# Cumulative decays, query latent and modulation blocks issued elsewhere in a two-layer hybrid diffusion backbone

## Chip, cores, metric

One core of a Trainium2 chip runs the whole program in one launch. The metric is the device time of that launch in microseconds (us). It is stated as the median of several runs.

## What is computed

The reference is a backbone of two layers (here called layer 0 and layer 1) over 512 latent tokens and 256 context tokens of width 1024. Cut to what the change touches, one layer is:

```python
mx = (silu(c) @ w_ada + b_ada)            # six modulation vectors: shift, scale, gate, twice
h  = rms_norm(x) * (1 + scale) + shift
p  = h @ w_in                             # columns: query latent, key/value latent, neighbourhood q k v,
                                          # DeltaNet q k v, gate z, two decay and two beta columns per head
mla = softmax_attention(rms_norm(q_latent) @ w_q_up, rms_norm(kv_latent) @ w_kv_up, ...)
na  = neighbourhood_attention(nq, nk, nv, bias)
q, k, v = silu(depthwise_conv(...));  g = -exp(a_log) * softplus(a + dt_bias)
gc  = cumsum(g) in each chunk             # decays exp(gc), exp(gc_last - gc), exp(gc_last)
dn  = gated_delta_rule(l2norm(q), l2norm(k), v, g, beta), both directions
dn  = rms_norm(dn) * silu(z)
x   = x + gate * (concat(mla, na, dn) @ w_out);   then a SwiGLU block with its own modulation
```

The context tokens go through the same weights in layer 0. In layer 1 they only serve as keys and values.

## The kernel before

Every matrix product with a large weight runs on TensorE in three passes of a rounded high part and a low part (`gemm`, L341). A weight tile of 128 output columns is loaded from memory into a buffer `wr`, split on ACT (`wh`, L216) and POOL (`wl`, L217), and multiplied with eight blocks of the normalised input (`hh`, `hl`). Two buffers of each exist. For the 512 latent columns a tile costs 24 matmuls of 512 columns, for the 256 context columns 24 of 256. The results of the input projection lie in three PSUM banks: two for latent accumulators (`x512`) and one for context accumulators (`x256`), so a second context product waits until the first one is read.

The source is written in an order of stages, and the Tile framework's scheduler then fixes the order of the instructions on each engine before the run. It walks a timeline of its own; where several instructions of an engine are ready on it, the one written earlier goes first. On the chip each engine runs its list in that order: an instruction that waits holds everything behind it. `tc.issue_after(x)` adds one constraint: the instructions in its block come behind `x` on the engine of `x`.

The stages of a layer, in the order in which they are written:

- the decay and beta columns (`TILE_AB`, L513), and from them `g`, a chain of some thirty small instructions on DVE and ACT, among them a series in L538 to L540. Its last step is L547.
- the cumulative decays (L553 to L563): five small fp32 products of `g` with constant triangles into one bank `gc`, two instructions each on PE, and five exponentials on ACT that give `egc`, `etail` and `egl`. The first reader is L620 in `gates`; the others are read in the scan.
- four key projections with their convolution (`conv("k", h)`, L484, L591), then the norms of the keys (`norms`, L568), the query and value projections with `gates` between them, the neighbourhood projections, and a triangular inverse in blocks.
- the tail (L977 to L986), an order written by hand in `TAIL` (L46): `z` is one gate tile (`do_z`, L786: projection, tanh on ACT, product on DVE at L791, a transfer of `z` to memory at L794), `k` the key/value latent (`do_kv`), `q` the query latent (`do_ql`, L762: two tiles, squares, their sum `sqs` on DVE at L771, six products with ones into `ms_q`, then the scale of the queries by L778, L780 to L783). The tanh of the last `z` is followed by a load of the activation table that holds ln and exp (`preload`, L182). Behind the tail the pools of the input (`h`), of the convolution buffers (`cvp`, which also holds `sqs`, `sq`, `thz` and `z`) and of the projection banks are closed, and others take their place.
- neighbourhood attention in 12 blocks in layer 0 and 8 in layer 1 (`attention`, L843). Ahead of each block `beside` (L1095) issues some steps of the DeltaNet scan and inverse (`DNS`), and in layer 0 two modulation blocks (`ADA`, L37). Then come the latent attention, the output projection and the SwiGLU block.

A modulation block (`ada_cols`, L220) loads 512 KB of `w_ada` into `wada`, multiplies it with the condition in eight products (`acc_ada`), copies the result to SBUF (`adarow`, L231, one buffer), and turns it into columns with a product per 128 values (`tr_ada`), to which DVE adds the bias (L236). In the first part of layer 0 four pairs of such calls stand ahead of the first norm; the 24 blocks beside the attention give the parts 2, 4 and 3, which are read from the output projection on.

POOL and DVE meet behind the tail: POOL prepares the block inverse with four products `Y` of 1024 columns (L941), DVE transposes strips (L925, L935) and does the softmax steps.

## Time and profile before

| | us |
|---|---|
| median of 3 runs | 2143.08 |
| lowest and highest run | 2142.63, 2143.99 |
| the profiled execution's own time | 2144.62 |
| its span, first to last instruction | 2142.5 |
| PE busy in the span | 1997.7 (93%) |
| DVE, ACT, POOL busy | 1178.1, 707.3, 839.9 |

PE is TensorE's matmuls, PEld its weight loads (they overlap PE), DVE is VectorE, ACT ScalarE, POOL GpSimd, SPq the queue of SyncE that issues transfers. A timeline row tells the start of an instruction from the span's start, its length, engine, source line, what it writes and reads, its shape, how many like it are merged, and in brackets how long its engine sat idle before it and which instruction released it. Every matrix product has the line of the helper, L104, so these are told apart by their tiles. The granted clock is the share of TensorE's full speed (1.00 is 2.4 GHz, 0.50 is 1.2 GHz) in a stretch.

### The profile page before, as it was taken

To read this page: it belongs to the slowest core of one execution; us is meant where nothing else is said; L and a number is where in the kernel's file an instruction comes from. 1 tells how busy PE (TensorE), PEld (TensorE's weight loads), DVE (VectorE), ACT (ScalarE), POOL (GpSimd) and SP (SyncE) were. 2 spreads that over 40 slices of the span, in tenths; PEclk is the share of its full clock that TensorE was granted. 3 is DMA by queue.
4 is the path that set the end of the run, shared out by engine and by line. 5 is a ranking of instruction groups with operands and counts; after the bars stand their busy time and mean duration, and the time that the engine had idled before them with its cause. 6 is when DMAs were issued, how large, how long until landed. Compare 5 with 4: busy or idle time off the path is not lost. (4 is left out here: it accounts for less than half of the span.)

```text
span 2142.5 us, 32149 instructions
## 1 busy us (share of the span) xinstructions
PE 1997.7 (93%) x12770; PEld 1692.0 (79%) x12770; DVE 1178.1 (55%) x2045; ACT 707.3 (33%) x1381; POOL 839.9 (39%) x664
## 2 busy tenths in 40 slices
PE   6899898998998999999999988868899889999998
PEld 4788687887787888888888876757787678888887
DVE  4889813667757457246344358893478654212123
ACT  5433223334544221122122344323344543222233
POOL 3467733103332222322222443884302352444444
PEclk9999998999999999999999999989899999999999
DMA  7324242443322334234432331334222232333332
GB/s 277 82 80 136 100 127 95 150 147 125 106 62 79 108 124 168 93 128 135 131 118 81 121 87 59 123 109 119 94 77 77 82 99 69 95 93 94 102 96 91
DMA packets 119278, 232.57 MB, mean 109 GB/s; under 512 B 30484, under 2 KB 55956, under 8 KB 119000
## 3 DMA queue, kind: packets, MB, share of 16 engines
q1 hardware_dynamic: 119128, 230.51, 34.1%
q8 instruction: 101, 1.65, 0.3%
q14 instruction: 49, 0.40, 0.1%
HBM read 199.46 MB, written 31.01 MB: 108 GB/s over the span
## 5 line engine op out<-in xcount | busy, mean ns | idle before, releaser
L217 POOL TENSOR_TENSOR wl<-wr,wh 128x1024 fp32r<-128x1024 f32 (+2 forms) x188 | 439.8, 2340 | 773.7 <-ACT wh L216 750.3
L216 ACT CAST wh<-wr 128x1024 fp32r<-128x1024 f32 (+2 forms) x190 | 193.6, 1019 | 730.1 <-PE acc_gu L104 289.4
L104 PE MATMUL acc_gu<-fh,wh 128*128 128x512 f32 (+1 forms) x1024 | 358.8, 353 | 9.6 <-ACT fh L304 8.7
L104 PE MATMUL acc_gu<-fl,wh 128*128 128x512 f32 (+1 forms) x1024 | 360.5, 353 | 4.1 <-DVE fl L305 4.1
L104 PE MATMUL acc_gu<-fh,wl 128*128 128x512 f32 (+1 forms) x1024 | 359.5, 352 | 0.0
L104 PE MATMUL acc_in<-hh,wh 128*128 128x512 f32 (+1 forms) x640 | 230.9, 365 | 25.3 <-DVE nkl L703 8.6
L104 PE MATMUL acc_in<-hl,wh 128*128 128x512 f32 (+1 forms) x640 | 230.3, 361 | 3.2 <-DVE hl L305 2.0
L104 PE MATMUL acc_in<-hh,wl 128*128 128x512 f32 (+1 forms) x640 | 227.3, 360 | 2.3 <-POOL wl L217 2.1
L104 PEld LDWEIGHTS acc_gu<-fh,wh 128*128 128x128 f32 x1024 | 193.9, 190 | 37.5 <-ACT fh L304 11.0
L1344 DVE TENSOR_TENSOR av<-acc_gu,av 128x768 f32<-128x768 f32 (+1 forms) x44 | 36.3, 825 | 337.0 <-PE acc_gu L104 329.8
L104 PEld LDWEIGHTS acc_gu<-fl,wh 128*128 128x128 f32 x1024 | 194.6, 190 | 30.2 <-DVE fl L305 4.3
L104 PEld LDWEIGHTS acc_gu<-fh,wl 128*128 128x128 f32 x1024 | 194.4, 190 | 26.3
L104 PEld LDWEIGHTS acc_in<-hh,wh 128*128 128x128 f32 x640 | 127.2, 200 | 52.8 <-DVE nkl L703 9.9
L104 PE MATMUL acc_d<-al,wh 128*128 128x512 f32 (+1 forms) x444 | 157.2, 354 | 0.0
L104 PE MATMUL acc_d<-ah,wh 128*128 128x512 f32 (+1 forms) x444 | 157.2, 354 | 0.0
L104 PE MATMUL acc_d<-ah,wl 128*128 128x512 f32 (+1 forms) x444 | 156.1, 354 | 0.0
L254 DVE CUSTOM_DVE_ANT_0 junk<-wada,scb 128x1024 f32<-128x1024 f32 x112 | 144.7, 1292 | 7.2 <-DMA wada<-w_adaT 4.4
L104 PEld LDWEIGHTS acc_in<-hl,wh 128*128 128x128 f32 x640 | 127.8, 200 | 24.8 <-DVE hl L305 4.6
L104 PEld LDWEIGHTS acc_in<-hh,wl 128*128 128x128 f32 x640 | 126.5, 200 | 21.0 <-POOL wl L217 3.6
L1362 DVE SCALAR_TENSOR_TENSOR xT<-acc_d,mod,xT 128x512 f32<-128x512 f32 (+1 forms) x76 | 46.5, 634 | 154.6 <-PE acc_d L104 154.6
L501 DVE SCALAR_TENSOR_TENSOR cy<-xp,cw,cy 128x770 f32<-128x770 f32 (+1 forms) x96 | 117.7, 1226 | 22.0 <-ACT cy L499 20.0
L1348 DVE TENSOR_TENSOR al<-av,ah 128x768 fp32r<-128x768 f32 (+1 forms) x44 | 100.4, 2282 | 35.1 <-ACT ah L1347 35.1
(391 smaller groups left out, 3957.8 us busy)
## 6 DMA issues: line engine op xcount, KB each, us to landing
wr<-w_gu SPq DMA_DIRECT2D x88, 512.0 KB, 3.5
wada<-w_adaT SPq DMA_DIRECT2D x56, 512.0 KB, 3.3
wr<-w_in SPq DMA_DIRECT2D x48, 512.0 KB, 3.7
wr<-w_dn SPq DMA_DIRECT2D x32, 448.0 KB, 3.4
wada<-w_ada SPq DMA_DIRECT2D x24, 512.0 KB, 3.3
wada<-w_ada SPq DMA_DIRECT2D x8, 1024.0 KB, 8.4
wr<-w_dn SPq DMA_DIRECT2D x16, 512.0 KB, 3.5
xT<-xT SPq DMA_DIRECT2D x16, 384.0 KB, 5.7
```

The lines of the kernel that those rows point to most:

```text
L104: nc.tensor.matmul(out, lhsT, rhs, start=start, stop=stop)
L216: S.copy(out=hi[:, sl], in_=raw[:, sl])
L217: eng.tensor_tensor(out=lo[:, sl], in0=raw[:, sl], in1=hi[:, sl].bitcast(F32), op=ALU.subtract)
L254: V.tensor_tensor_reduce(out=junk, in0=w, in1=scb[:, s], scale=1.0, scalar=0.0, op0=ALU.mult, op1=ALU.add, accum_out=mod[l][:, part, j, s: ...
L501: stt(out=y[:, :wid], in0=xp[:, j:j + wid], scalar=w_(j), in1=y[:, :wid], op0=ALU.mult, op1=ALU.add)
L1344: tt(out=av[:, :nT], in0=accs[1][:, :nT], in1=av[:, :nT], op=ALU.mult)
L1348: after.append(tt(out=l_[:, :nT], in0=av[:, :nT], in1=h_[:, :nT].bitcast(F32), op=ALU.subtract))
L1362: stt(out=xT[:, m, st_], in0=acc, scalar=mod[l][:, 5, m, s:s + 1], in1=xT[:, m, st_], op0=ALU.mult, op1=ALU.add)
```

## The change

Three edits.

1. The five products of the cumulative decays and their exponentials are written behind the four key projections, and the products are bound behind the last matmul of those projections (`last["mm"]`). This holds in both layers.
2. In layer 0 the tail is `zkqzzz` instead of `zzzzkq`: one gate tile, the key/value latent, the query latent, three gate tiles.
3. A modulation block beside the attention returns its second half (`turn`: `tr_ada`, the bias, and the scale) instead of running it. It is run after the first half of the next block, and bound behind that block's last matmul; the last one runs after the loop. `adarow` has two buffers. The calls ahead of the first norm run both halves at once, as before.

```diff
--- before.py
+++ after.py
@@ -43,7 +43,7 @@
 PRE0, LATE = True, ()
 ROW = lambda S, V: S.copy
 HLP = ([(k, 1) for k in range(8)], [], [(k, 1) for k in (0, 2, 4, 6, 7)], [])
-TAIL = ["zzzzkq", "kzzqzz"]
+TAIL = ["zkqzzz", "kzzqzz"]
 INV = ((3, 4), (5, 2))
 WV = ((6,), (23,))
 MR = 2
@@ -101,7 +101,7 @@
 
 
 def mm(nc, out, lhsT, rhs, start=True, stop=True):
-    nc.tensor.matmul(out, lhsT, rhs, start=start, stop=stop)
+    return nc.tensor.matmul(out, lhsT, rhs, start=start, stop=stop)
 
 
 def mm3(nc, out, l, r, start=True, stop=True):
@@ -226,19 +226,22 @@
         acc = bank("acc_ada")
         for k in range(KD):
             g = 32 * (k % 4)
-            mm(nc, acc[g:g + 32, 0:nb * P].rearrange("p (j c) -> p j c", j=nb), sc[:, k], w[:, :, k], k < 4, k >= 4)
-        row = sb.tile([P, nb * P], F32, tag="adarow", name="adarow", bufs=1)
+            last["ada"] = mm(nc, acc[g:g + 32, 0:nb * P].rearrange("p (j c) -> p j c", j=nb), sc[:, k], w[:, :, k], k < 4, k >= 4)
+        row = sb.tile([P, nb * P], F32, tag="adarow", name="adarow", bufs=2)
         (V.tensor_copy if slot is wp else ROW(S, V))(out=row, in_=acc[:, 0:nb * P])
-        res = bank("tr_ada")
-        for b in range(nb):
-            mm(nc, res[:, 2 * b:2 * b + 2], row[:, b * P:(b + 1) * P], C("sum4"))
-        js = slice(j0, j0 + nb)
-        tt(out=mod[l][:, part, js], in0=res[:, 0:2 * nb].rearrange("p (j s) -> p j s", s=2), in1=bc(bada[:, l, part, js], 2), op=ALU.add)
-        if part in (1, 4):
-            i = part // 4
-            t1 = sb.tile([P, nb, 2], F32, tag="adat", name="adat", bufs=1)
-            V.tensor_scalar(out=t1, in0=mod[l][:, part, js], scalar1=1.0, scalar2=None, op0=ALU.add)
-            tt(out=gs[l][:, i, js], in0=t1, in1=bc(gm[:, l, i, js], 2), op=ALU.mult)
+
+        def turn():
+            res = bank("tr_ada")
+            for b in range(nb):
+                mm(nc, res[:, 2 * b:2 * b + 2], row[:, b * P:(b + 1) * P], C("sum4"))
+            js = slice(j0, j0 + nb)
+            tt(out=mod[l][:, part, js], in0=res[:, 0:2 * nb].rearrange("p (j s) -> p j s", s=2), in1=bc(bada[:, l, part, js], 2), op=ALU.add)
+            if part in (1, 4):
+                i = part // 4
+                t1 = sb.tile([P, nb, 2], F32, tag="adat", name="adat", bufs=1)
+                V.tensor_scalar(out=t1, in0=mod[l][:, part, js], scalar1=1.0, scalar2=None, op0=ALU.add)
+                tt(out=gs[l][:, i, js], in0=t1, in1=bc(gm[:, l, i, js], 2), op=ALU.mult)
+        return turn
 
     def ada_rows(todo, sb, after):
 
@@ -347,7 +350,7 @@
                 o = acc[:, st.start - c0:st.stop - c0]
                 mm(nc, o, wh[:, w], xh[k][:, st], k == 0, False)
                 mm(nc, o, wh[:, w], xl[k][:, st], False, False)
-                mm(nc, o, wl[:, w], xh[k][:, st], False, k == nk - 1)
+                last["mm"] = mm(nc, o, wl[:, w], xh[k][:, st], False, k == nk - 1)
 
 
     es_x = ExitStack()
@@ -399,7 +402,7 @@
 
     if nx is None:
         nx = e.open_norm(l, A_)
-        pre = lambda k: k % 2 or [e.ada_cols(l, p, k, 2, eb, nx.sb, nx.sb) for p in (1, 0)]
+        pre = lambda k: k % 2 or [e.ada_cols(l, p, k, 2, eb, nx.sb, nx.sb)() for p in (1, 0)]
         pre(0)
         rss = e.rstd_of(xT, eb, nx.sb, both)
         for k in range(KD):
@@ -549,18 +552,6 @@
     S.activation(out=beta, in_=ab[:, :, 8:16], func=AF.Exp, scale=-1.0)
     V.tensor_scalar(out=beta, in0=beta, scalar1=1.0, scalar2=None, op0=ALU.add)
     V.reciprocal(out=beta, in_=beta)
-
-    egc, etail, egl = sc6(), sc6(), sc6()
-    tp = eb("gc")
-    gf = g.rearrange("p c x -> p (c x)")
-    for i, nm in enumerate(("u_f", "u_b", "v_f", "v_b", "ones")):
-        mm(nc, tp[:, 48 * i:48 * i + 48], C(nm), gf)
-    tpv = lambda i: tp[:, 48 * i:48 * i + 48].rearrange("p (c x) -> p c x", x=8)
-    for d in range(2):
-        ds_ = slice(4 * d, 4 * d + 4)
-        S.activation(out=egc[:, :, ds_], in_=tpv(d)[:, :, ds_], func=AF.Exp)
-        S.activation(out=etail[:, :, ds_], in_=tpv(2 + d)[:, :, ds_], func=AF.Exp)
-    S.activation(out=egl, in_=tpv(4), func=AF.Exp)
     V.tensor_scalar(out=sml[:, 12:13], in0=sml2[:, 19:20], scalar1=0.5, scalar2=None, op0=ALU.mult)
 
     t2 = lambda nm: sb.tile([P, 512], F32, tag="t2", name=nm, bufs=5)
@@ -590,6 +581,19 @@
 
     for h in range(4):
         conv("k", h, kT[:, h])
+
+    egc, etail, egl = sc6(), sc6(), sc6()
+    tp = eb("gc")
+    gf = g.rearrange("p c x -> p (c x)")
+    with tc.issue_after(e.last["mm"].ins):
+        for i, nm in enumerate(("u_f", "u_b", "v_f", "v_b", "ones")):
+            mm(nc, tp[:, 48 * i:48 * i + 48], C(nm), gf)
+    tpv = lambda i: tp[:, 48 * i:48 * i + 48].rearrange("p (c x) -> p c x", x=8)
+    for d in range(2):
+        ds_ = slice(4 * d, 4 * d + 4)
+        S.activation(out=egc[:, :, ds_], in_=tpv(d)[:, :, ds_], func=AF.Exp)
+        S.activation(out=etail[:, :, ds_], in_=tpv(2 + d)[:, :, ds_], func=AF.Exp)
+    S.activation(out=egl, in_=tpv(4), func=AF.Exp)
     st4, rk = [sb.tile([P, 6, 4], F32, name=nm) for nm in ("st4", "rk")]
     norms("k", t2, st4, rk, True)
     irk = sc3()
@@ -1092,13 +1096,22 @@
 
     ada_bank = lambda name: (psV if ADA_T == "i" else psD).tile([P, 512], F32, tag=ADA_T, name=name, bufs=1)
 
+    turns = []
+
+    def turn_last():
+        if turns:
+            with tc.issue_after(e.last["ada"].ins):
+                turns.pop()()
+
     def beside(ada, sb):
 
         for _ in range(next(dn_n, 16)):
             next(dn, lambda: 0)()
         for _ in range(next(ada, 0) if l == 0 else 0):
             i = next(ada_n)
-            e.ada_cols(0, (2, 4, 3)[i // KD], i % KD, 1, att_bank if ADA_T == "T" else ada_bank, sb, e.wp)
+            turn = e.ada_cols(0, (2, 4, 3)[i // KD], i % KD, 1, att_bank if ADA_T == "T" else ada_bank, sb, e.wp)
+            turn_last()
+            turns.append(turn)
 
 
 
@@ -1106,6 +1119,7 @@
         beside(ada, sn)
         if next(na, None) is None:
             break
+    turn_last()
     es_w.close()
     es_si.close()
     es_na.close()
```

## Rows read from the trace of the kernel before

**Rows 1.** The page's part 1: busy time, share of the span, instructions.

```profile
PE 1997.7 (93%) x12770; PEld 1692.0 (79%) x12770; DVE 1178.1 (55%) x2045; ACT 707.3 (33%) x1381; POOL 839.9 (39%) x664
```

**Rows 2.** Windows at the end of layer 0's projections: length, busy us of PE, PEld, DVE, ACT, POOL, granted clock, DMA.

```profile
290.00:351.00 61.00, 61.00 (x376) 52.69 (x375) 7.20 (x12) 19.98 (x31) 14.33 (x8) 1.00 0.34 110
351.00:370.00 19.00, 11.19 (x67) 9.97 (x65) 13.17 (x32) 3.79 (x14) 10.65 (x7) 0.69 0.39 130
370.00:382.00 12.00, 12.00 (x76) 9.46 (x77) 4.49 (x16) 3.51 (x11) 0.00 (x0) 0.50 0.18 55
382.00:490.00 108.00, 107.91 (x1372) 90.93 (x1371) 72.26 (x237) 35.79 (x123) 13.21 (x21) 1.00 0.49 163
```

**Rows 3.** Timeline, PE, layer 0's seam: start, length, [idle before <- releaser].

```profile
354.75 2.52 PE L104 MATMUL ms_q<-cst,sqs 128*128 128x2 f32 x12 [3.63 <-DVE sqs L771]
357.81 0.56 PE L104 MATMUL tr_ada<-cst,adarow 128*128 128x2 f32 x2 [0.55 <-DVE adarow L231]
...
359.31 2.08 PE L104 MATMUL yp<-vp,Y 128*128 128x128 f32 x8
...
365.54 0.59 PE L104 MATMUL tr_ada<-cst,adarow 128*128 128x2 f32 x2 [3.62 <-DVE adarow L231]
```

**Rows 4.** Timeline, DVE, the same stretch.

```profile
352.19 2.41 DVE L771 TENSOR_TENSOR sqs<-sqs,sq 128x768 f32<-128x768 f32 x1
357.30 0.16 DVE L778 TENSOR_SCALAR sml<-ms_q 128x6 f32<-128x6 f32 x1 [2.70 <-PE ms_q L104]
...
362.10 2.29 DVE L782 TENSOR_SCALAR sml<-sml 128x6 f32<-128x6 f32 x1
...
365.40 0.68 DVE L1031 TENSOR_TENSOR w<-yp,scal 128x512 f32<-128x512 f32 x1
```

**Rows 5.** Timeline, POOL, the same stretch.

```profile
351.45 2.34 POOL L941 TENSOR_TENSOR Y<-strips,cst 128x1024 f32<-128x1024 f32 x1
357.40 6.96 POOL L941 TENSOR_TENSOR Y<-strips,cst 128x1024 f32<-128x1024 f32 x3 [3.61 <-PE ms_q L104]
```

**Rows 6.** Timeline, PE, layer 1's tail and seam.

```profile
1520.43 0.95 PE L104 MATMUL ms_q<-cst,sqs 128*128 128x2 f32 x8
...
1542.42 1.11 PE L885 MATMUL tp_na<-cst,pr 128*128 128x128 f32 x4 [4.07 <-DVE pr L880]
```

**Rows 7.** Windows, layer 1's seam (columns as in rows 2).

```profile
1529.00:1546.00 17.00, 9.34 (x60) 7.68 (x59) 14.47 (x24) 6.05 (x14) 12.15 (x8) 0.70 0.40 131
```

**Rows 8.** Timeline, ACT, the last gate tile of layer 0.

```profile
324.86 0.38 ACT L790 ACTIVATE thz<-acc_in 128x256 f32<-128x256 f32 x1
325.26 1.28 ACT L182 ACT_TABLE_LOAD   x1
```

**Rows 9.** The tile z of layer 0: its vector step, and its transfer to memory.

```profile
L791 DVE SCALAR_TENSOR_TENSOR z<-thz,acc_in x8: 420/554/691, 297.0 to 325.3; 128x512 f32<-128x512 f32 x4, 128x256 f32<-128x256 f32 x4
...
DMA to landing us min/median/max: 2.8/3.1/3.1
```

**Rows 10.** Timeline, ACT, layer 1's tail: an activation table.

```profile
1522.18 1.28 ACT L781 ACT_TABLE_LOAD   x1
```

**Rows 11.** Timeline, PE, layer 0's key projections.

```profile
79.13 1.31 PE L104 MATMUL gc<-scal,cst 128*128 128x48 f32 x10 [0.98 <-DVE scal L547]
81.73 0.48 PE L104 MATMUL acc_in<-hh,wh 128*128 128x256 f32 x1 [1.29 <-ACT xp L495]
```

**Rows 12.** Windows of layer 0 behind the key projections (columns as in rows 2).

```profile
84.00:136.00 52.00, 51.32 (x277) 40.81 (x277) 38.98 (x52) 24.81 (x39) 16.96 (x24) 0.99 0.18 61
136.00:262.00 126.00, 111.50 (x627) 93.63 (x626) 118.15 (x156) 36.32 (x57) 105.93 (x113) 0.95 0.34 111
```

**Rows 13.** Timeline, PE, layer 1: the cumulative decays.

```profile
1292.69 0.28 PE L104 MATMUL acc_in<-hh,wl 128*128 128x256 f32 x1
1292.81 0.40 PE L104 MATMUL acc_in<-hh,wh 128*128 128x512 f32 x1
...
1308.42 2.37 PE L104 MATMUL gc<-scal,cst 128*128 128x48 f32 x10 [6.68 <-DVE scal L547]
```

## The prediction

> **What bounds the kernel.** I read the page's shares first, then TensorE's waits stage by stage, then the timelines of the other engines in the stretches where it waits, and last the granted clock there. PE is busy 93% of the span [rows 1], so a change of order can win only what PE idles or runs at half clock. Most stages leave nothing: in layer 0's tail PE is busy 61.00 of 61 us at clock 1.00, and in the attention stretch 107.91 of 108 [rows 2]. Between them lies a seam. From 351 to 370 us PE is busy 11.19 of 19 us at a mean clock of 0.69, and from 370 to 382 it has no gap but runs wholly at 0.50 [rows 2]. That makes 7.8 us idle, and 2 x 0.31 x 19 + 12 = 23.8 us at 1.2 GHz. All three edits should be read against this seam and against one stall in layer 1.
>
> In the seam PE waits 3.63 us for `sqs`, runs `ms_q` at half clock in 2.52 us, waits 0.55 and later 3.62 us for `adarow` [rows 3]. Behind `ms_q` hang others too: POOL's last three `Y` wait for it 3.61 us [rows 5], because `sqs` lies in memory that they take over. In layer 1 PE stands 6.68 us before the decays [rows 13].
>
> **The query latent moves ahead of three gate tiles.** The same matmuls run, in another order.
> - The wait for `sqs` (3.63 us) goes: the sum on DVE takes at most 2.41 us [rows 4], and a gate tile's projection stands behind it, a seventh of the tail's 61 us or 8.7 us of PE work [rows 2]. Layer 1 already has gate tiles behind its query latent, and there `ms_q` starts without an idle bracket [rows 6]. Gain 3.6 us. If the scheduler places `ms_q` before that cover, the wait stays.
> - `ms_q` itself runs at full clock: eight took 0.95 us in layer 1 [rows 6], so twelve take 1.4 instead of 2.5. Gain 1.1.
> - Something else is last now. Behind the last gate matmul come tanh of the context part (0.38 us), the table load (1.28) [rows 8] and DVE's product (0.42) [rows 9]; only then are the bank and the buffers free. In the old order all three lay under the latents' projections. The sum is 2.1 us; if the next stage needs only the bank, without the load, it is 0.8; if it needs memory that `z` holds until its transfer lands (3.1 us [rows 9]), it is 0.4 + 0.4 + 3.1 = 3.9, plus the loads of the scan, which SP issues in order behind this transfer. I take 2.1, since the freed resource nearest to the first rows of the seam is the bank and ACT must load the table before its first exp.
> - ln and exp of the two latents now lie between tanh steps. In layer 1, where they do, exp cost another load of 1.28 us [rows 10]. Up to five more loads are 6.4 us of ACT, which is busy only 19.98 of the tail's 61 us [rows 2]: nothing, as long as the casts of the next weights are not the ones delayed; then 1.28 each.
> - The transfers of three gate tiles and the weight loads move with their steps on SP; seven weight tiles are loaded before and after. Nothing.
>
> **The modulation blocks.** 24 blocks issue the same instructions. The first wait (0.55) goes, since the next block's eight products stand before the turn. The second (3.62) is only partly the block's own: the `adarow` copy stood on DVE behind L782, which took 2.29 us, and L1031, which PE's next step needs, ended only at 366.1 [rows 4]. L782 belongs to the query latent and leaves the seam with it. So of 3.62 I count 2.3. Together 2.9 us; bounds 0.5 and 4.2. In the 108 us behind the seam PE has 0.1 us of idle time [rows 2], so the other blocks win nothing there; the second `adarow` is only memory. Each turn takes a bank of the attention's three one block later; I count nothing, and up to 0.1 us for each of 24 if a score tile has to wait for it, 2.4 in all.
>
> **DVE against POOL.** L782 has six columns. The like-shaped L778 took 0.16 us, L782 2.29, inside POOL's three `Y` from 357.40 to 364.36 [rows 4, 5]. In layer 1 a transpose waits 4.07 us for DVE's `pr`, in a seam where POOL is busy 12.15 of 17 us [rows 6, 7]. With `ms_q` gone, the three `Y` no longer wait 3.61 us, and meet the first softmax steps. I add 1.5 us, between 0 and the 4.07 of layer 1, nearer the low end because the steps they meet are few.
>
> [...]
>
> **The clock.** The 12.00 us of work behind the seam at 0.50 would take about 6 at full clock. In layer 1's seam 2 x 0.30 x 17 = 10.2 us are at half clock [rows 7], against 23.8 here. With less idle time I expect about half of that difference, 6.8 us less at 1.2 GHz, worth some 3.0 us. Bounds 0 and 6.
>
> **The decays.** In layer 0 `gc` stands in a hole that stays: PE waits 0.98 us, runs 1.31, and waits 1.29 for ACT's `xp`, which does not depend on it [rows 11]. Moved behind the projections, the 1.31 us lands in a stretch where PE is busy 51.32 of 52 us [rows 12]. Behind that, DVE is the fuller engine (118.15 of 126 us, PE 111.50), so part is taken up. I add 0.7; bounds 0 and 1.3. The exponentials are first read in `gates`, which comes behind the projections in either order. In layer 1 the last context matmul of the key projections is issued at 1292.69, and other projections follow it before `gc` [rows 13]. So `gc` is already behind them there; the new bound is met by the old order, `g` comes no earlier, and I count 0 of the 6.68.
>
> **Sum**: -3.6 - 1.1 + 2.1 - 2.9 + 1.5 - 3.0 + 0.7 = -6.3 us. Against the profiled execution's 2144.62 that is 2138.3; the median stands 1.54 lower, so 2143.08 - 6.3 = 2136.8, said as **2137.0**. 0.2%, about what a measurement can tell from no change, is 4.3 us: faster means below 2138.8, slower above 2147.4.
>
> **Rivals.**
> 1. *Layer 1's stall goes too.* If writing `gc` later makes the scheduler put more query projections before it, the 6.68 us is covered, and `gc` runs in 1.31 instead of 2.37 us [rows 11, 13]: 7.7 more, 2129. For it: work is there, since projections resume right after. Against: nothing that `g` or PE's readiness depends on has moved.
> 2. *The seam only moves.* [...] Then the waits are replaced, and the clock with them; only `ms_q` and `gc` differ: 2143.08 - 1.1 + 0.7 = 2142.7. [...] For it: all of POOL's 9.3 us of `Y` fall together right behind the last matmul.
> 3. *Slower: the half clock lasts.* Today PE goes back to full clock at 382, after 12 us without a gap at 0.50 [rows 2]. If the new seam, thinner by the 2.5 us of `ms_q`, leaves PE at 1.2 GHz for 12 us of busy work more, that costs 6; with idle time unchanged, 2142.7 + 6 = 2148.7. It decides if the clock is not back within some 31 us of the last projection matmul. Against: in layer 1's seam 10.2 of 17 us are at half clock, not all of it [rows 7].
>
> **Chances.** Forecast 0.45, of its own 2132 to 2141; rival 1 0.18, rival 2 0.25, rival 3 0.12. Of the forecast two thirds lie below 2138.8 (0.30), all of rival 1 (0.18), a little of rival 2 (0.04): faster 0.52. Slower 0.14: rival 3 with a little of rival 2. Same 0.34. The range reaches from rival 1 with the larger clock gain, 2129 - 3 = 2126, to rival 2 with the decays at their upper bound and 0.7 of the bank's 1.8 (0.6 + 0.7 more), 2144; rival 3 is left out.
>
> **What would show it.** `ms_q` without an idle bracket, in the middle of a gate projection; no `tr_ada` wait over 1 us; the end of the half clock nearer than 25 us to the last projection matmul; `gc` of layer 0 behind the last key tile, with no idle time there; `gc` of layer 1 still behind a wait near 6.7 us. Wrong if layer 1's wait is gone, if DVE steps of 2.3 us fill the seam, or if waits of PE for weights appear in the tail.

## The result, and the profile after

The changed kernel takes 2177.51 us (median of 4 runs, 2169.67 to 2191.92) against 2143.53 for the kernel before (median of 4): 1.0157 times the time, 95% interval 1.0128 to 1.0187. Forecast were 2137.0, and at most 2144. The profiled execution took 2170.37, its span is 2168.6. Part 1 of its page answers to [rows 1]: the same 12770 matmuls, 11 us more of PE.

```profile
PE 2008.9 (93%) x12770; PEld 1699.6 (78%) x12770; DVE 1183.3 (55%) x2045; ACT 712.2 (33%) x1385; POOL 839.7 (39%) x664
```

**The seam that the edits aim at ends earlier in this execution, by the clock.** Windows of the changed kernel, columns and stretches as in [rows 2]:

```profile
290.00:351.00 61.00, 59.63 (x365) 50.47 (x363) 9.30 (x15) 23.92 (x37) 13.82 (x6) 1.00 0.30 99
351.00:370.00 19.00, 12.20 (x93) 10.79 (x92) 10.01 (x28) 5.37 (x13) 11.13 (x8) 0.73 0.53 163
370.00:382.00 12.00, 12.00 (x125) 9.86 (x123) 6.61 (x25) 5.12 (x17) 1.04 (x1) 1.00 0.47 149
382.00:490.00 108.00, 105.50 (x1321) 86.86 (x1320) 73.46 (x231) 37.35 (x123) 19.34 (x23) 1.00 0.52 167
```

The 12 us from 370 on, at 0.50 before, are at full clock, and half clock between 351 and 382 falls from 23.8 to 2 x 0.27 x 19 = 10.3 us. This counts a clock of either 1.00 or 0.50: in the kernel before, 34 of the 38 windows of 1 us from 348 to 386 read one of the two, and four lie between. At 1.00 products of 512 columns start 0.227 us apart there and those of 256 0.120 (from 299.7 on), so 256 columns more take 0.107 us, 2.4 columns per ns; at 0.50 products of 256 start 0.213 us apart (from 373.7 on), 1.2 columns per ns. The prediction's GHz can be read as an estimate from these rates, with one column per clock. TensorE's idle time does not fall. The tail and the seam together, first in the kernel before, then in the changed kernel:

```profile
290.00:382.00 92.00, 84.19 (x516) 72.12 (x516) 24.86 (x60) 27.28 (x55) 24.98 (x14) 0.87 0.33 107
290.00:382.00 92.00, 83.83 (x579) 71.12 (x577) 25.92 (x68) 34.41 (x66) 25.99 (x15) 0.94 0.37 119
```

PE idles 7.8 us before and 8.2 us after. And the clock differs between executions of one list. Two runs that are described below have in this stretch PE's list of the kernel before (first line, no edits at all) and that of the changed kernel (second line; its one difference, products in layer 1 that nobody reads, comes later):

```profile
290.00:382.00 92.00, 84.23 (x562) 72.44 (x560) 26.15 (x64) 28.02 (x57) 26.02 (x15) 0.91 0.37 116
290.00:382.00 92.00, 83.51 (x518) 70.26 (x516) 22.62 (x57) 32.24 (x59) 24.95 (x14) 0.87 0.31 100
```

So the old list ran here at 0.87 and 0.91, the new one at 0.94 and 0.87. That the edits raise the clock is not shown.

The timeline of PE in the changed kernel, against [rows 3]:

```profile
331.99 1.40 PE L104 MATMUL ms_q<-cst,sqs 128*128 128x2 f32 x12
...
355.43 0.38 PE L104 MATMUL tr_ada<-cst,adarow 128*128 128x2 f32 x2 [0.56 <-DVE adarow L231]
360.87 1.44 PE L104 MATMUL yp<-vp,Y 128*128 128x128 f32 x5 [5.06 <-DMA vp<-d_v]
...
375.03 0.38 PE L104 MATMUL tr_ada<-cst,adarow 128*128 128x2 f32 x2
```

`ms_q` has no idle bracket and full clock; the second turn no longer waits. But the scan's first product `yp` (five of its eight matmuls fall into the window that was read) now waits 5.06 us for `vp`, and starts at 360.87, not 359.31 [rows 3]. The queue of SP in the changed kernel shows why: the load of `vp` is issued behind the transfer of the last gate tile. In the kernel before it was issued at 348.64.

```profile
355.31 0.53 SPq L798 DMA_DIRECT2D d_z<-z  x1
355.88 0.64 SPq L1011 DMA_DIRECT2D vp<-d_v  x1
```

In the tail, where PE had no gap before [rows 2], it now waits for the cast of a weight (what waited, for what; us in total, times, longest):

```profile
PE acc_in L104 <- ACT wh L216: 1.1, 1, 1.1
```

The decays of layer 0 and of layer 1, PE's timeline, against [rows 11, 13]: no idle time ahead of the first; the second behind the same wait.

```profile
95.48 1.21 PE L104 MATMUL gc<-scal,cst 128*128 128x48 f32 x10
...
1314.82 2.37 PE L104 MATMUL gc<-scal,cst 128*128 128x48 f32 x10 [6.69 <-DVE scal L550]
```

**Then time is lost, in two places.** The last product of layer 0's neighbourhood attention (`o_na`) starts at 482.2, before at 492.5. These 10.3 us are not all gained: in the changed kernel 56 matmuls of the scan (16 `ks`, 16 `qs`, 8 each of `yp`, `sp` and `oa`) stand behind this `o_na` that stood ahead of it. By 382 us the changed kernel is 64 matmuls in front, by 492.5 us only 3. First the kernel before, then the changed one (the number behind PE's busy time):

```profile
0.00:382.00 382.00, 332.81 (x2100) 275.20 (x2101) 239.71 (x378) 137.64 (x248) 195.60 (x199) 0.93 0.40 126
0.00:492.50 492.50, 443.22 (x3494) 368.51 (x3496) 314.02 (x619) 174.54 (x373) 211.31 (x221) 0.94 0.42 135
```

```profile
0.00:382.00 382.00, 328.24 (x2164) 271.56 (x2164) 240.89 (x386) 144.37 (x259) 196.63 (x200) 0.96 0.41 130
0.00:492.50 492.50, 435.36 (x3497) 360.03 (x3498) 316.38 (x619) 182.64 (x384) 217.18 (x224) 0.97 0.43 138
```

The first product of layer 0's feed-forward (`acc_gu`), which has the same number of matmuls ahead of it in both, starts at 683.7, before 677.2: 6.5 us late. Layer 1 starts 6.4 us late (`gc`), its `ms_q` 5.4 late, its last `o_na` 23.5 late (1627.1 against 1603.6), its first `acc_gu` 25.5 late, its end 26.1 late. Two windows of the kernel before, from layer 0's last `o_na` to its first `acc_gu`, and from layer 1's first to its last `o_na`:

```profile
492.50:677.20 184.70, 164.68 (x1084) 136.41 (x1080) 123.38 (x265) 85.65 (x227) 65.33 (x54) 0.96 0.26 81
1532.60:1603.60 71.00, 65.64 (x823) 57.30 (x824) 54.99 (x138) 27.09 (x87) 15.60 (x12) 0.93 0.28 85
```

The same two of the changed kernel:

```profile
482.20:683.70 201.50, 174.10 (x1139) 145.97 (x1135) 132.14 (x274) 87.18 (x227) 64.04 (x54) 0.95 0.26 78
1537.70:1627.10 89.40, 83.57 (x807) 71.44 (x808) 55.79 (x138) 25.54 (x84) 15.59 (x12) 0.71 0.23 69
```

Length times granted clock is an estimate of what a stretch would take at full clock; twice (1 - clock) times length is its half clock. In layer 1 the stretch, with 16 matmuls fewer in it, would take 63.5 us in place of 66.0, but 51.9 us of it run at half clock in place of 9.9: by this estimate the whole loss there is the clock's. In layer 0 it is 191.4 in place of 177.3. PE is busy 9.4 us longer there, which includes the 56 matmuls moved into it (some 7 us, an estimate from a run below that has them too), and idles 27.4 us in place of 20.0. The waits of PE there, in the changed kernel (engine, line, tile, what it waited for; us in total, times, longest):

```profile
PE acc_gu L104 <- ACT fh L307: 5.8, 1, 5.8
PE yp L104 <- DVE rr L1030: 5.5, 3, 3.0
PE tp_mla L1227 <- DVE pr L1223: 3.9, 2, 2.3
PE s_mla L104 <- ACT qh L1138: 3.0, 1, 3.0
PE sp L104 <- DVE w L1035: 2.0, 2, 1.2
```

And in the kernel before, where no wait on `qh` stands and `tp_mla` waits 0.6 us:

```profile
PE acc_gu L104 <- ACT fh L304: 6.7, 1, 6.7
PE yp L104 <- DVE rr L1026: 3.8, 2, 3.3
PE acc_mv L104 <- ACT wkh L1124: 1.7, 1, 1.7
```

No source line of these two stages is changed. What differs is the order in which the scheduler lists their instructions. The edits change what is ready when on the scheduler's timeline, and so it sorts the steps of the scan (`yp`, `sp`, `ks`, `qs`, `oa`) and of the inverse (`pp`, `yq`) otherwise between the attention's products. The listed orders show it: over the kernel before, the changed one and those with one or two of the edits, eight in all, PE has seven orders in layer 0's latent attention, five in layer 1's tail and neighbourhood attention, two in layer 1's latent attention. Writing `gc` later changes nothing in layer 1 by itself: a kernel with that edit in layer 1 alone is listed exactly as the kernel before.

### The profile page after: what moved, and what is told of

The parts are those of the page before. It is cut to its first block, busy times and chain, and to the rows that moved or that the text cites. A ratio compares the mean times of both kernels' runs of the same rounds, so it can differ in the third digit from the quotient of the medians.

```text
span 2168.6 us, 32148 instructions
## 1 busy us (share of the span) xinstructions
PE 2008.9 (93%) x12770; PEld 1699.6 (78%) x12770; DVE 1183.3 (55%) x2045; ACT 712.2 (33%) x1385; POOL 839.7 (39%) x664
## 5 line engine op out<-in xcount | busy, mean ns | idle before, releaser
L104 PEld LDWEIGHTS acc_gu<-fh,wh 128*128 128x128 f32 x1024 | 194.1, 191 | 36.6 <-ACT fh L307 10.1
```

The lines of the kernel that those rows point to most:

```text
L104: return nc.tensor.matmul(out, lhsT, rhs, start=start, stop=stop)
```

## Experiments

**The three edits, alone and in pairs.** Theory R: nothing is paid where the edits stand; the later stages, sorted anew, cost it. Rival A: each edit has a price of its own. The first has the first edit's hunks alone:

```diff
+    with tc.issue_after(e.last["mm"].ins):
+        for i, nm in enumerate(("u_f", "u_b", "v_f", "v_b", "ones")):
+            mm(nc, tp[:, 48 * i:48 * i + 48], C(nm), gf)
```

> The decays edit alone. Its issue orders are those of the kernel before in all of layer 1's first stage and differ in layer 0's head, its latent attention, and layer 1's tail and neighbourhood attention. Theory R (the edits cost nothing where they stand, the loss comes from later stages that the scheduler sorts anew, different from kernel to kernel): layer 0 up to the last pass of its neighbourhood attention +1 us or less against before; what is left, up to 10 us either way, arises in layer 0's latent attention and layer 1's neighbourhood attention alone; 2138 to 2155 us. Rival A (each edit has a cost of its own, and the costs add up to the 34 us): a fixed share of the 34 us, at the place of the edit, so that layer 0's key projections end 5 us later or more; about 2150 us.

The second only

```diff
-TAIL = ["zzzzkq", "kzzqzz"]
+TAIL = ["zkqzzz", "kzzqzz"]
```

> Only the order of layer 0's tail is changed (query latent ahead of the gate tiles). Theory R: the query latent loses its wait of 3.6 us and its half clock, the seam ends 3 to 6 us earlier; layer 0's latent attention is issued in the same order as in the kernel with the decays edit alone, so it gains or loses the same there as that one within 2 us; layer 1's tail has an order of its own: the outcome there is open, up to 20 us lost, and if so in a half-clock stretch; 2136 to 2160 us. Rival A: the last gate tile's work stays exposed at the seam, 5 to 10 us lost there, none in layer 1; about 2150 us.

The third only the later turns:

```diff
-            e.ada_cols(0, (2, 4, 3)[i // KD], i % KD, 1, att_bank if ADA_T == "T" else ada_bank, sb, e.wp)
+            turn = e.ada_cols(0, (2, 4, 3)[i // KD], i % KD, 1, att_bank if ADA_T == "T" else ada_bank, sb, e.wp)
+            turn_last()
+            turns.append(turn)
```

> Only the turns of the modulation blocks are made one block later. Its layer 1 is issued in the order of the kernel before throughout. Theory R: layer 1 from its first decay matmul to the end takes what it takes before, within 2 us; the waits of the turns (2.9 us and more) go from layer 0's neighbourhood attention; its latent attention has an order of its own, up to 10 us either way; 2134 to 2150 us. Rival A: the second row buffer and the later turns cost by themselves, 10 us or more in layer 0's neighbourhood attention; 2155 us.

The fourth has the first two diffs,

> Decays and tail order, without the turns. Its layer 1 is issued in the order of the kernel before throughout. Theory R: layer 1 from its first decay matmul to the end takes what it takes before, within 2 us, although each of the two edits alone sorts that layer anew; 2134 to 2152 us. Rival A: the sum of what the two edits cost alone (first and second kernel of this call), wherever they cost it.

a later one the second and third,

> Tail order and turns, without the decays edit. Theory R (nothing is paid where the edits stand, each kernel's later stages are sorted anew): the end of layer 0's neighbourhood attention is 5 to 12 us earlier than before; from there to the end the time is its own draw, not the sum of the two edits' draws; 2140 to 2165 us. Rival A (costs add up): 9 us plus 11 us over before, 2164 us, and the third edit adds the rest.

and another the first and third.

> Decays and turns, without the new tail order. Theory R: the end of layer 0's neighbourhood attention 5 to 10 us earlier than before; layer 1's tail in the order of the kernel with the decays edit alone, so that its neighbourhood attention takes 74 to 84 us as there; 2140 to 2165 us in all. Rival A: 11 us plus 11 us over before, 2166 us or more.

Measured (ratio to the kernel before with its interval; starts in us; "half" is the half clock from layer 1's first to its last `o_na`; profiled executions):

| kernel | ratio | last o_na, layer 0 | last yp, layer 0 | first acc_gu, layer 0 | half |
|---|---|---|---|---|---|
| before | 1 | 492.5 | 526.5 | 677.2 | 9.9 |
| changed | 1.0157 [1.0128, 1.0187] | 482.2 | 531.9 | 683.7 | 51.9 |
| decays | 1.0064 [1.0042, 1.0085] | 487.3 | 521.4 | 671.1 | 27.9 |
| order | 1.0052 [1.0028, 1.0076] | 485.0 | 518.5 | 670.6 | 10.3 |
| turns | 1.0056 [1.0037, 1.0075] | 485.0 | 525.8 | 676.7 | 28.0 |
| decays, order | 1.0010 [0.9997, 1.0024] | 485.9 | 520.1 | 673.8 | 28.0 |
| order, turns | 1.0109 [1.0070, 1.0149] | 505.2 | 555.0 | 705.0 | 28.0 |
| decays, turns | 1.0083 [1.0062, 1.0105] | 486.8 | 527.5 | 678.4 | 10.3 |

Rival A's sums miss in two cases of four: decays and order cost 0.64% and 0.52% alone and 0.10% together, decays and turns 0.83% where the sum is 1.20%. In the other two they fit (order and turns 1.09% against 1.08%, all three 1.57% against 1.72%), so these runs alone don't refute it; those with a given order, below, do.

The column of the last `o_na` compares like with like only in the rows without turns: with the turns alone, and with decays and turns, 40 matmuls of the scan come behind it instead of ahead, with order and turns and in the changed kernel 56. In the rows without turns it comes 5.2 to 7.5 us early. Decays with order has PE's list of the kernel before in that stage, and from 391.6 us on every `o_na` is 6.6 us earlier. But 4.3 us of that come with no edit at all: the kernel without edits and with the new order behind (second row of the next table) has the same list from there to 478 us, and is 4.3 us early throughout.

Theory R fails in part too. The turns alone (2155.30 us) and order with turns (2168.91) lie above its ranges. The kernels with the turns, and with decays and order, have layer 1 listed on every engine as before. R said that they need the same time there within 2 us; from layer 1's `gc` to its first `acc_gu` they take 456.3 and 455.6 us, before 452.3, and run 28 us at half clock, not 10. Order is not all that sets the clock. And with order and turns alone, 505.2 is late: 40 us at half clock in layer 0's neighbourhood attention.

**Filling the seams.** That idle PE time drops the clock is an assumption; in the kernel before the 12 us at 0.50 stand behind 7.8 us of idle time [rows 2]. If it holds, products that nobody reads should keep the clock up. In layer 1's seam, ahead of the first `o_na` and of the second block's `tp_na`, on the changed kernel and on decays with order:

```diff
+FILL = (5, 4, 9)
...
+                    for _ in range(FILL[1 + j] if (l, pair, qt) == (1, 0, 1) else 0):
+                        mm(nc, h4(tp), ident, bc1(ident, 4))
...
+                for _ in range(FILL[0] if (l, pair, qt) == (1, 0, 0) else 0):
+                    mm(nc, h4(o_), ident, bc1(ident, 4))
```

> The changed kernel, and in layer 1's seam 18 matmuls of the identity on itself (results never read) where its TensorE stands idle for 2.3, 1.5 and 3.6 us around the first tiles of the neighbourhood attention. Theory C (the seam's idle time drops the clock, and how long it then stays at half, 17 to 51 us in the kernels so far, sets most of the spread in layer 1's neighbourhood attention): half clock between its first and last o_na falls from 51 us to 15 us or less, and that stage from 89 us to 64 to 70 us; 2148 to 2165 us. Rival O (the new order of the work there costs the time, whatever the clock): the stage keeps 80 us or more; 2168 to 2185 us.

> Decays and tail order without the turns, with the same 18 matmuls in layer 1's seam. Theory C: half clock in layer 1's neighbourhood attention falls from 27 us to 15 us or less, the stage from 78 us to 64 to 70 us; 2132 to 2142 us, below the kernel before. Rival O: 2143 to 2150 us, as without the matmuls.

The changed kernel with the fill: 1.0112 [1.0058, 1.0165], half clock in that stretch 3.3 us, its length still 82.3 us; decays and order with it: 1.0054 [1.0035, 1.0073], worse than without. Both medians (2166.13 and 2155.86) lie in neither theory's range. The windows from layer 1's first to last `o_na`, first of decays with order, then of the same with the fill:

```profile
1527.10:1604.80 77.70, 72.48 (x822) 63.03 (x824) 54.64 (x138) 27.34 (x87) 15.59 (x12) 0.82 0.27 78
```

```profile
1524.80:1605.50 80.70, 80.70 (x868) 63.15 (x868) 57.13 (x147) 29.63 (x90) 17.94 (x15) 1.00 0.26 79
```

In this execution, the fastest of ten, the half clock is gone, 28 us to 0, and nothing is won: the 18 products take some 16 us of PE (the first five run from 1524.8 to 1529.3) and the first `yp` comes at 1542.7, not 1537.8. So the fill was made smaller, and one put ahead of layer 0's first `yp`:

```diff
-FILL = (5, 4, 9)
+FILL = (3, 2, 4)
+FILL0 = 5
...
+        for _ in range(FILL0 if (l, d, x) == (0, 0, 0) else 0):
+            mm(nc, h4(yp), ident, bc1(ident, 4))
```

on decays with order (first without `FILL0`),

> Decays and tail order, and in layer 1's seam 9 unread matmuls in place of 18, sized to the idle time (2.7, 1.8 and 3.6 us). Theory C (the idle seam drops the clock, the half clock that follows costs the time): no half clock in layer 1's neighbourhood attention, its first yp 4 to 5 us earlier than with 18, the stage from there 60 to 64 us; 2132 to 2145 us. Rival D (each kernel's order of the later work is a draw of its own, and the order before happened to be a good one): 2150 us or more, half clock or not.

> As the kernel before it, and in layer 0's seam 5 unread matmuls (4.5 us) ahead of the first yp, where TensorE waits 5 us for vp. Theory C: the half clock of 10 us at that seam (31 us in other runs) goes too, 5 us less than the kernel before it; 2127 to 2141 us. Rival D: 2150 us or more.

on the changed kernel,

> The changed kernel with both seams filled (5 and 9 unread matmuls). Theory C: no long half clock behind either seam; the 10 to 25 us by which executions of the changed kernel differ shrink to 10 or less; what is left over the kernel before is the 17 us of layer 0's latent attention, if that is its order: 2140 to 2158 us. Rival D: 2160 us or more, with the same spread.

and on the kernel before.

> The kernel before with the same two fills and no other edit. Theory C: it loses the half clock behind its seams too (24 us in layer 0, 10 in layer 1), and gains 5 to 15 us: 2128 to 2138 us. Rival D: any edit in the seam leads to another order, 2145 to 2165 us.

Ratios, in this order: 1.0076 [1.0048, 1.0103], 1.0070 [1.0047, 1.0093], 1.0120 [1.0064, 1.0176], 1.0025 [1.0005, 1.0044]. All four miss theory C's numbers and lie in rival D's; three still have 13 us of half clock in layer 1's stretch. The fills also sort the rest anew, so these runs don't separate clock from order. The last one is of use: its layer 0 is through early, with last `yp` at 520.8 and first `acc_gu` at 666.6, 10.6 us ahead of before.

**The order alone.** Each instruction of the later stages is bound behind its predecessor in a given list. This adds no work, only the order in which an engine lists what it has: the kernel without edits and with the changed kernel's order has 1139 and 807 matmuls in its two windows below, as many as the changed kernel.

```diff
     with tile.TileContext(nc, schedule_with_timeline_sim=True) as tc:
         emit(tc, aps, out)
+        named = {i.name: i for i in nc.cur_bb.bb.instructions}
+        for chain in json.loads(zlib.decompress(base64.b85decode(PINNED))):
...
+            for p_, q_ in zip(chain, chain[1:]):
+                tc.add_manual_dep(named[f"I-{q_}"], f"I-{p_}", mybir.DependencyInfo(mybir.DependencyClass.NoSync, mybir.DependencyReason.DATA), reason="pinned")
```

The lists come from the compiled kernel before, or from the changed one. First all three edits with the old order from the last pass of layer 0's neighbourhood attention on; then the kernel before with the new order there (the run without edits named above); then the edits with the old order in layer 1 only; and the changed kernel once more.

> All three edits, with each engine's instructions behind the last pass of layer 0's neighbourhood attention pinned to the order that they have in the kernel before; the work is the same. Theory D (the new order of the later stages costs the time, the edits themselves don't): the seam's gain of 10 us at the end of layer 0's neighbourhood attention is kept in part, layer 0's latent attention takes 178 to 188 us in place of 201, layer 1's neighbourhood attention 70 to 78 us in place of 89; 2130 to 2148 us. Rival S (the edits themselves, by what they leave late or by the clock behind the seam): 2160 us or more.

> The kernel before with none of the edits, and behind the last pass of layer 0's neighbourhood attention each engine pinned to the order of the changed kernel. Theory D: layer 0's latent attention 10 us or more longer than before, and layer 1's neighbourhood attention 80 us or more: 2155 to 2180 us. Rival S: as before, 2139 to 2150 us.

> All three edits, and only from layer 1's first input projection on each engine pinned to the order of the kernel before. Theory D: layer 0 as in the changed kernel (its latent attention 198 to 203 us, layer 1's decays 6 us later than before), layer 1 from there within 8 us of before; 2146 to 2165 us. Rival S: 2165 us or more.

> The changed kernel again, for its spread on this chip. Theory D: 2160 to 2192 us, its executions 10 us or more apart, and that difference in the clock alone (span times mean clock equal within 8 us). Rival S: the same time; this run only places the others.

| kernel | ratio | median us | last yp, layer 0 | first acc_gu, layer 0 | half |
|---|---|---|---|---|---|
| edits, old order behind | 1.0015 [0.9992, 1.0039] | 2143.26 | 522.4 | 673.4 | 10.1 |
| no edits, new order behind | 1.0143 [1.0113, 1.0173] | 2176.11 | 537.1 | 690.4 | 51.9 |
| edits, old order in layer 1 | 1.0069 [1.0046, 1.0091] | 2154.86 | 535.6 | 688.8 | 9.9 |
| changed kernel again | 1.0128 [1.0104, 1.0152] | 2172.26 | 536.3 | 687.9 | 51.9 |

This decides it, for theory D. The unedited kernel with the changed kernel's later order is as slow as the changed kernel; the edits with the old order cost nothing that can be told (at most 0.39%, by the interval). They gain nothing that can be told either: the 6.3 us of the forecast would be a ratio of 0.9971, below the interval. Windows (layer 0's latent attention to the feed-forward, and layer 1's neighbourhood attention), first of the edits with the old order, then of the new order without the edits:

```profile
481.90:673.40 191.50, 171.52 (x1139) 142.68 (x1136) 128.28 (x274) 85.33 (x227) 65.32 (x55) 0.97 0.27 83
1529.20:1601.70 72.50, 66.23 (x822) 57.71 (x824) 55.18 (x138) 26.91 (x87) 15.57 (x12) 0.93 0.27 83
```

```profile
485.00:690.40 205.40, 178.82 (x1139) 150.31 (x1135) 133.64 (x273) 88.08 (x228) 67.43 (x56) 0.92 0.26 79
1543.40:1632.90 89.50, 83.62 (x807) 71.44 (x808) 55.80 (x138) 25.57 (x84) 15.60 (x12) 0.71 0.23 69
```

The second line of the second fence is that of the changed kernel almost to the digit, clock 0.71 included. Theory D said 178 to 188 us for the first stretch of the old order; it took 191.5. PE is busy 171.52 us in it, before 164.68: the 6.8 us more are the size of the 56 matmuls that lie behind the last `o_na` here, and the stretch is longer by as much. In the third kernel layer 1's `gc` came 10.9 us late where D said 6, and the changed kernel's executions were only 7.6 us apart here, not 10 or more.

**Where in layer 1, and a version faster than both.** Same means. First the unread products ahead of layer 0's first `yp` on the kernel before, with layer 1 in the old order:

```diff
+FILL0 = 5
...
+            mm(nc, h4(yp), ident, bc1(ident, 4))
...
+        for chain in json.loads(zlib.decompress(base64.b85decode(PINNED))):
```

> The kernel before with 5 unread matmuls in layer 0's seam, and from layer 1's first input projection on each engine pinned to the order of the kernel before. Theory D: layer 0 as in the kernel with both fills (its feed-forward starts 5 to 11 us earlier than before), layer 1 as before within 8 us: 2130 to 2140 us, below both kernels. Rival E (what an order gains in layer 0 is lost again to the clock, whose half stretches differ from one execution to the next): 2141 to 2150 us.

Then the changed kernel with layer 1 in the old order up to its first `yp`, and in its own from there (the same lines with another list):

> The changed kernel with layer 1 up to its first yp pinned to the order of the kernel before and from there on to the changed kernel's own. If the order behind the seam makes the half-clock stretches of 41 and 10 us, they stay, layer 1's neighbourhood attention takes 85 us or more, 2164 to 2176 us. If the order ahead of the seam makes them, by the moment at which the idle time falls, at most 27 us of half clock in a row, 70 to 82 us for that stage, 2148 to 2163 us.

The first takes 2136.97 us, 0.9973 [0.9952, 0.9994]: faster than both kernels, though by little. Layer 0's feed-forward starts at 665.8 and layer 1 keeps the 10 us of half clock. The unread products also sort layer 0 anew; whether this order or the clock gives the gain was not separated:

```profile
486.20:665.80 179.60, 162.64 (x1084) 134.99 (x1080) 122.91 (x264) 86.41 (x226) 61.74 (x52) 0.98 0.25 80
1523.30:1595.80 72.50, 66.22 (x823) 57.77 (x824) 55.18 (x138) 26.91 (x87) 15.56 (x12) 0.93 0.28 83
```

The second takes 2155.61 us, 1.0075 [1.0049, 1.0101], and its layer 1 stretch, although listed as in the changed kernel, loses the long half clock:

```profile
1539.70:1612.30 72.60, 67.01 (x807) 57.64 (x808) 54.94 (x138) 25.25 (x84) 15.59 (x12) 0.93 0.28 84
```

So, as far as one trace and eight executions show, the 51.9 us hang on the order ahead of layer 1's seam, not on that behind it. The other traces agree: the three with the changed kernel's list ahead of that seam all have 51.9, and all the others without a fill there 28 or less. Ahead of the seam the changed kernel issues the blocks of the inverse later: its 32 `pp` products start at 1515.91, 10.0 us ahead of `ms_q`, in the kernel before at 1508.33, 12.1 ahead. Whether this step or another does it was not tried.

## Why the prediction was wrong

**Right, at the place of the edits.** `ms_q` loses its wait and takes the 1.40 us that were said. The second turn's wait is gone; the first stays with 0.56 us, where it was said to go. `gc` in layer 0 has no idle time, and what follows is not later: the first product of the neighbourhood's values (`acc_v`) comes at 248.1, before at 248.7 (said: 0.7 later). In layer 1 it keeps its wait, 6.69 us.

**The first step that failed: that the waits go.** The sum took out 6.5 us of waits (3.6 for `sqs`, 2.9 for the blocks) and put in 2.1 for the last gate tile and 1.5 for DVE's steps beside POOL's `Y`, so PE should have idled 2.9 us less. It idles 8.2 us between 290 and 382, before 7.8. The term of 2.1 was mis-sized: in its place stands the wait of 5.06 us for `vp`. The text had seen this end: `z` in memory until its transfer lands, and the loads of the scan behind it on SP. That is what came, `vp` is issued 7.2 us later. POOL waits for the same transfer, in the changed kernel:

```profile
360.31 4.64 POOL L945 TENSOR_TENSOR Y<-strips,cst 128x1024 f32<-128x1024 f32 x2 [1.04 <-DMA d_z<-z]
```

Behind it come 0.8 us for `w` and 0.4 for `LP`, and in the tail the 1.1 us for the cast `wh`, a wait that the prediction put at nothing and named as a sign of being wrong. The first `yp` is 1.6 us later than before; but the kernel without edits and with the new order behind has it at 360.74, so this is no loss that the edits are shown to cause.

**The clock term** stood at 6.8 us less of half clock. From 290 to 382 the two profiled executions differ by 2 x (0.13 - 0.06) x 92 = 12.9 us, worth 6.4, and that is about all by which the attention behind the seam is early with decays and order (6.6 us, at the same mean clock of 0.94). But in the kernel without edits and with the new order behind, whose list here is the old one, the same window has 2 x 0.09 x 92 = 16.6 us of half clock, and in the changed kernel with a fill in layer 1, whose list here is the new one, 23.9, as much as before. One trace of each kernel is not enough to count such a term; had the total come out, it would have been luck.

**The second, which makes the loss: that all later work only shifts.** The sum ends at 490 us and takes the rest as given. The text knew that the scheduler sorts by a timeline of its own and used that for `ms_q` and `gc`, not for what comes after. Measured: the last `yp` 5.4 us later than before (531.9), where the old order gives 522.4, and layer 1 slower by 19 us (from `gc` to `acc_gu` 471.4 against 452.3). Of the 29 us between the changed kernel, run again, and the kernel before beside it (mean spans 2169.8 and 2141.0), 20 are clock and 9 are not: span times (1 - mean clock) is 95.5 us against 75.6, span times clock 2074.3 against 2065.4.

What the end of layer 0 follows may be the scan: in the kernels of the two tables the first `acc_gu` comes 150 to 154 us behind the last `yp` (with a fill 146 to 161), while the last `o_na` lies between 482 and 505. This is read from the starts; a run that hurries the scan alone was not made.

**The rivals.** That layer 1's wait goes: no. That the seam only moves: yes for the idle time, through a transfer and not through steps of DVE, and its 2142.7 us are close to the 2143.26 of the edits with the old order. That the half clock lasts: not in layer 0's seam of the changed kernel's own trace, where 31 us from the last projection were the mark (its last product starts at 354.02, and from 370 the clock is full). It does in the run with a fill in layer 1, whose list is the same up to there: the last projection product starts at 355.00, and the clock is still low here:

```profile
382.00:390.00 8.00, 8.00 (x50) 6.67 (x51) 2.09 (x9) 0.65 (x2) 1.04 (x1) 0.54 0.35 105
```

And it lasts in layer 1's seam, which no edit touches. The third was right that a half clock can last, here 40 us in a row (windows of 1 us from 1539 to 1579 read 0.50); that its place would be layer 0's seam was not.

On DVE beside POOL: in layer 0's new seam one softmax step took 1.38 us, where the median of its line is 0.15, while POOL ran two `Y` from 360.31 to 364.95, and PE shows no wait for it:

```profile
363.59 1.38 DVE L882 TENSOR_TENSOR st<-st 128x1 f32<-128x1 f32 x1
```

In the changed kernel's layer 1 four `Y` take 9.45 us from 1537.69 on, 2.36 each, and three steps of DVE that start in this time take 2.30 to 2.33, about one `Y` each, where the median of these two lines is 0.15 (L882) and 0.48 us (L884). What makes these steps long was not shown. The kernel before has the same wait there (4.07 us [rows 6], now 3.61), so it is no part of the difference.

```profile
1540.31 2.33 DVE L884 TENSOR_SCALAR pr<-pr,st 128x512 f32<-128x512 f32 x1
1542.56 2.30 DVE L882 TENSOR_TENSOR st<-st 128x1 f32<-128x1 f32 x1
1545.09 2.33 DVE L884 TENSOR_SCALAR pr<-pr,st 128x512 f32<-128x512 f32 x1
```

**Open** stays what in the order ahead of layer 1's seam keeps the clock down, and why the same list of layer 1 has 10 us of half clock in four kernels and 28 in two (decays, and decays with turns, also share one list there, and have 28 and 10). Open is also how the changed kernel loses its lead of 64 matmuls between 382 and 492.5 us, where PE shows hardly a wait.

## What to carry to other kernels

Where a scheduler orders the instructions, an edit need not stay local: compare the listed orders of all engines behind it before a gain is counted, and hold the old order there to see what the edit itself is worth. When waits are to go from a seam, add up the idle time of the whole seam afterwards, since others can take their place; here a load that stood behind a moved transfer did. A mark in the trace, such as the last product of a stage, can itself be moved by the edit: count the work done up to it. A clock that falls in one short seam can stay low far behind it (here for 51.9 us of the 89.4 from layer 1's first to its last `o_na`), and differs between executions of one list (0.94 and 0.87 from 290 to 382), so a single trace of each kernel is no measure of it.

## What was not expected of the hardware

One stretch of work, layer 1's neighbourhood attention, would take 63 to 69 us at full clock in all kernels without a fill there, and ran 10, 28 or 52 us of its time at half clock. And the clock fell from 1.00 to 0.50 without a wait of PE that the profile shows. Windows in the middle of layer 0's neighbourhood attention, in the changed kernel with the fill of layer 1 (listed as the changed kernel up to there):

```profile
422.00:428.00 6.00, 6.00 (x75) 4.60 (x76) 3.58 (x12) 1.08 (x4) 1.85 (x3) 1.00 0.72 239
428.00:434.00 6.00, 6.00 (x92) 4.36 (x89) 3.45 (x13) 4.29 (x19) 1.09 (x5) 0.70 0.26 93
434.00:440.00 6.00, 6.00 (x37) 4.91 (x37) 3.78 (x13) 1.05 (x4) 0.60 (x1) 0.50 0.55 153
```

In the changed kernel itself 382 to 490 us is at 1.00 throughout, with the same list. The last `o_na` came at 508.3 in the one and 482.2 in the other: 26 us between two executions of the same list. Of seven traces with this list of PE, five have it between 481.9 and 486.5 and two at 505.2 and 508.3. The rows do not show what made the clock fall; the ends of matmuls in the profile are modelled.
